# A third of block 2's first modulation on VectorE beside linear attention, and the context's second-layer path dealt in larger portions

## The chip, the cores and the metric

The kernel runs on one core of one Trainium2 chip, in one launch. The metric is the device time of the whole program in microseconds. Three runs of the kernel before took 3452.48, 3447.66 and 3446.35 us, median 3447.66 us.

## The reference, cut to what matters

Block 1 is a mixing block (differential attention and gated linear attention, called GLA below, then a router and 32 experts), whose shifts and scales come from `w_ada`. Block 2 has two layers. Each computes a modulation vector from the conditioning for the main tokens (512) and one for the context tokens (256), and both then pass through the same weights:

```python
s_c, s_ctx = silu(c), silu(c_ctx)[None]
for i in range(2):
    mod = (s_c @ w_mod[i] + b_mod[i])[:, None, :]             # 6 x 1024 columns
    sh1, sc1, gt1, sh2, sc2, gt2 = split(mod, 6)
    mod_c = (s_ctx @ w_mod[i][:, :n_mod_c] + b_mod[i][:n_mod_c])
    h  = rms_norm(x, g_norm1[i]) * (1 + sc1) + sh1
    hc = rms_norm(ctx, g_norm1[i]) * (1 + mc[1]) + mc[0]
    p, pc = h @ w_in[i], hc @ w_in[i][...]
    ...                                                       # three attention branches, merge, MLP
```

Of `mod`, the first third (shift and scale of the first norm, columns 0 to 2047, which the kernel counts as 16 columns of 128) is what a path needs to start.

## The kernel before, in words

A matrix is split into a high and a low part (tiles `wh`, `wl`, `h`), and each product is three matmuls, L195 to L197 (`mm`). The modulations are the exception: `mods_group` (L326) multiplies the raw weights. A group is a third of a modulation, 32 matmuls (8 rows of the contraction by 4 column blocks) of 128x32 by 128x512, line L339, tile `mod`; column block j writes partitions 32j to 32j+31. The tile is copied (`modr`), transposed four times (`modt`) and added to the bias. Weights `wm` come by one 256 KB DMA a matmul on SyncE's queue, into tiles of the tag `at` (9 buffers) or `t2`.

Work is written by generators that yield a cost, and `weave` advances the one that is least far in its own time (cost divided by the stream's speed). What comes out is then put in an order on each engine when the program is built, and each engine keeps to it. Stages, by the time of the profile:

- 0 to 135 us, start: first third of block 1's modulation (mod0), norms, projections. 135 to about 270: GLA (`gla`, chains over 16 chunk steps through `S`, `gqd`, `zb`), woven with projections and with groups 1 and 2 of mod0 (`mods`, tag `at`).
- to 365: attention heads 0 to 2. With head 3 (`hd == 3`, L750) the stream `ctx` begins, which runs block 2's context path of layer 0, `path(0, 256)`, beside the rest of block 1 (project, route, experts, combine). Ahead of it stands `opening()`: group 0 of block 2's modulation of layer 0 (`mods2(0, "t2", (0,))`), which the path needs; groups 1 and 2 (`later`) follow when it is done.
- 1330 to 1450: the experts end (tile `yp`) and `combine` begins; the rest of `ctx` fills there.
- 2055 to 2431: `mlp` of `path(0, 512)`. Beside it run `mods2_cols(1, ...)`, which computes layer 1's whole modulation on VectorE, column by column (48 columns; two products of 128x512 with a running sum for each row of conditioning, L1217, tile `wc`; a column of the first 16 for both rows, of the others for one), and, once 16 columns are done, `fill`: `path(1, 256)`, which gives only keys and values of the context for layer 1 (tiles `ck`, `kv`, `mkr`, `mk`). `FILL_SPEED` and `COL_COST` set in which proportion.
- from 2431: `path(1, 512)`. Its norm (`ss` sums squares, `rs` is the inverse root, `rb` spreads it, then eight pairs of `nt` and `h`) is woven with what is left of `fill`, and its first projections take `h`.

Of the kernel before, what the change touches and what calls it, by code (L numbers as in the profile page):

```python
# [14 lines left out]
P = 128  # L15
# [15 lines left out]
FIRST = 70.0  # L31
JOIN = 75.0
NP = 3
FILL_SPEED = 0.15
COL_COST = 5.5
PRO_SPEED = 0.3
ROUTE_SPEED = 0.5

# [42 lines left out]
def weave(main, back=()):  # L81


    every = list(main) + list(back)
    for s in every:
        s.t = 0.0
    while any(not s.done for s in main) or any(s.hold for s in every):
        live = [s for s in every if not s.done]
        held = [s for s in live if s.hold]
        if held:  # L90
            live = [s for s in live if s.hold or not s.weights]
        if all(s.done for s in main):
            live = held
        yield abs(min(live, key=lambda v: v.t).step())


def drain(gen):
    for _ in gen:
        pass


def chain(*gens):
    for g in gens:
        yield from g


class Gen:
# [263 lines left out]
    def run(self):  # L371
        nc, tc = self.nc, self.tc
        one, two = "1" in self.parts, "2" in self.parts
        if one:
            xs = self.load_x(self.A["xT"], 512, "xx")
            s0 = self.cond(self.A["cc"], "mod0s")
        self.ident = self.const("c_ident")
        self.ones = self.cc(P)
        nc.vector.memset(self.ones, 1.0)
        dram = self.ctx.enter_context(tc.tile_pool(name="dram", bufs=1, space=bass.MemoryType.DRAM))  # L380
        self.xs_dram = [dram.tile([KD, P, 512], F32, name=f"xres{i}") for i in range(3)]
        self.ctx_dram = [dict(kna=dram.tile([4, P, 512], F32, name=f"kna{i}"), vna=dram.tile([2, P, 512], F32, name=f"vna{i}"),
                              kml=dram.tile([8, 96, 512], F32, name=f"kml{i}"), vml=dram.tile([2, P, 512], F32, name=f"vml{i}"))
                         for i in range(2)]
        self.v_dram = [dram.tile([512, 512], F32, name=f"vloc{i}") for i in range(2)]
        self.xctx_dram = dram.tile([KD, P, 256], F32, name="xctx")
        self.Hd = [dram.tile([512, 512], F32, name=f"Hd{c}") for c in range(2)]
        self.Id = dram.tile([1024, 1], I32, name="Id")
        self.Yd = dram.tile([NE * CAP + OVF * CAP, D], F32, name="Yd")
        ctx = []  # L390
        if two:
            place = lambda n: self.place(n)
            first = Stream(self.mods2(0, "t2", (0,), place))

            def rest():
                while not first.done:
                    yield 1
                yield from self.mods2(0, "t2", (1, 2), place)

            def opening():  # L400
                while not first.done:
                    yield first.step()

            later = Stream(rest(), 1.0, False)
            ctx = [Stream(chain(opening(), self.path(0, 256, before=later))), later]
        for s in ctx:
            s.speed = 0.5
        if two and not one:
            self.second_start()
        if one:  # L410
            project = self.front(ctx, xs, s0)
        else:
            self.xs_dram[0] = self.A["t_x"]
        if one:
            for gen, speed, held in ((project, PRO_SPEED, True), (self.route(), ROUTE_SPEED, False), (None, 0, 0),
                                     (self.experts(), CTX_SPEED, None), (self.combine(), TAIL_SPEED, None)):
                if gen is None:
                    self.branch()
                    continue
                for s in ctx:  # L420
                    s.speed = speed
                drain(weave([Stream(gen, 1.0, bool(held), (lambda: tc.high_priority(PRIOR)) if held is not None else None)], ctx))
        if two:
            self.rest = ctx
            self.fill = [Stream(self.path(1, 256), FILL_SPEED)]
            drain(self.path(0, 512))
            drain(self.path(1, 512))
        else:
            xs = self.load_x(self.xs_dram[0], 512, "xo")
            for k in range(KD):  # L430
                nc.sync.dma_start(self.out[k], xs[k])


    def front(self, ctx, xs, s0):
        nc, A, tc = self.nc, self.A, self.tc
# [84 lines left out]
        w = self.load_split(W[3], 256)  # L520
# [108 lines left out]
        def dv():  # L629
            for i in range(6):  # L630
                V[i] = self.t2("dv")
            for c in range(2):
                yield from row_tiles(6 + c, V, c * 256)

        gr = [None] * 4
        def gates():
            for i in range(4):
                gr[i] = self.t2("gr")
            for c in range(2):
                w = self.load_split(W[4 + c], 256)  # L640
                for t in range(4):
                    ps = self.mm()
                    self.rows(ps[:, :256], h, t, w)
                    self.silu2(gr[t][:, c * 256:(c + 1) * 256], ps[:, :256], 256)
                    yield 2.6 if t == 3 else -2.6
# [15 lines left out]
        def qk(hd):  # L661
            w = self.load_split(W[8 + hd], 256)
            q, k = self.pairs(2, 512, "dqk")
            kc = self.pairs(1, 256, "dkc")[0]
            for m, hl in ((0, q), (1, k)):
                ps = self.mm()
                self.colsT(ps, w, m, h)
                x = self.t2("rx")
                self.copy_act(x, ps, scale=1.0 if m else 0.125)
                yield -5.1  # L670
                pr = self.mm()
                nc.tensor.matmul(pr, rot, x, start=True, stop=True)
                t1 = self.t2("ry")
                nc.vector.tensor_tensor(t1, pr, sin, op=OP.mult)
                nc.gpsimd.tensor_tensor(x, x, cos, op=OP.mult)
                nc.vector.tensor_tensor(x, x, t1, op=OP.add)
                self.split(*hl, x)
                yield -1
            ps = self.mm()
            self.colsT(ps[:, :256], w, 1, hc)  # L680
            self.split(*kc, ps[:, :256])
            QK[hd] = q, k, kc
            yield 2.6
# [57 lines left out]
            yield 0.5  # L741

        mods = Stream(chain(*[self.mods_group(mod, s0, A["w_ada"], g, "at", lambda n: self.place(n)) for g in (1, 2)]), MOD_SPEED, False)
        self.place = self.dd
        drain(weave([Stream(gla(), 1.0, False), Stream(chain(gates(), dv(), qk(0)), 1.2)], [mods]))
        drain(mods.gen)
        self.place = self.mm
        for hd in range(4):
            drain(weave([Stream(attend(hd), 1.0, False), Stream(chain(gate_norm() if hd == 0 else (), qk(hd + 1) if hd < 3 else ()), 1.2)],
# [445 lines left out]
        self.s2 = self.cond(A["cc2"], "mod2s")  # L1195
        self.mod2 = [self.mods(A["b_mod"][L], f"mod2{L}") for L in range(2)]

    def mods2_cols(self, L, cost):

        nc = self.nc  # L1200
        bt, mod = self.mod2[L]
        junk = self.t2("junk")
        rows = [[self.load(self.at("crow")[:, :512], self.A["c2_rows"][c, h]) for h in range(2)] for c in range(2)]
        for s in rows[0] + rows[1]:
            nc.scalar.activation(junk, s, AF.Tanh, scale=0.5)
            nc.vector.scalar_tensor_tensor(s, junk, 1.0, s, op0=OP.add, op1=OP.mult)
        yield 1
        for j in range(48):
            w = [self.at("wc")[:, :512] for h in range(2)]
            for h in range(2):  # L1210
                nc.gpsimd.dma_start(w[h], self.A["w_mod_t"][j, h])
            if j == 16:
                rows.pop()
            for c, row in enumerate(rows):
                to, beg = mod[:, j, c:c + 1], bt[:, j:j + 1]
                for h in range(2):
                    nc.vector.tensor_tensor_reduce(junk, w[h], row[h], 0.5, beg, OP.mult, OP.add, to)  # L1217
                    beg = to
            self.mod2_cols = j + 1
            yield cost  # L1220

    def mods2(self, L, tag, groups=range(3), place=None):
        for g in groups:
# [12 lines left out]
    def path(self, L, n, side=None, before=None):  # L1236
# [197 lines left out]
            yield from s.gen  # L1434
        back = ()
        if lat and L == 0:
            cols, fill = Stream(self.mods2_cols(1, COL_COST), 1.0, False), self.fill[0].gen
            self.mod2_cols = 0

            def later():  # L1440
                while self.mod2_cols < 16:
                    yield 1
                yield from fill

            back = self.fill = [Stream(later(), FILL_SPEED), cols]
# [376 lines left out]
def layout(inp):  # L1822
# [3 lines left out]
    f = np.float32  # L1826
# [42 lines left out]


    A["w_mod"] = modw(x["w_mod_2"][0])
    A["w_mod_t"] = ca(x["w_mod_2"][1].T.reshape(48, P, 2, 512).transpose(0, 2, 1, 3))
    A["c2_rows"] = ca(np.repeat(np.stack([x["c_2"][0], x["c_ctx_2"]]).reshape(2, 2, 1, 512), P, 2))
    A["b_mod"] = np.stack([tiles(x["b_mod_2"][i]) for i in range(2)])
    for i in range(2):
# [104 lines left out]
```

## Time and profile before

| | us |
|---|---|
| three runs | 3452.48, 3447.66, 3446.35 |
| median | 3447.66 |
| profiled execution | 3450.65 |
| its span | 3448.7 |
| TensorE busy | 3274.5 |
| VectorE busy | 1776.7 |
| ScalarE busy | 1242.7 |

The profiled execution is 2.0 us longer than its span and 3.0 us above the median. The mean granted TensorE clock is 0.972. Busy shares are averages over the stages; a stage's limit is read from that stage.

### The profile page before, as it was taken

Reading aid. Unit: us, or ns where it says so; the run is one execution under the profiler, and the core shown is the slowest. Engines: PE = TensorE matmul, PEld = TensorE weight load, DVE = VectorE, ACT = ScalarE, POOL = GpSimd, SP = SyncE. Lnnn points to the kernel's source line nnn. Section 1 sums busy time; section 2 is a strip of 40 time slices with the busy share of each in tenths; the row PEclk is TensorE's granted clock in tenths of the full one; section 3 lists DMA queues with packets and bytes.
Section 4 is the critical chain, followed back from the end, with each engine's and each line's share of the span. In section 5 each row is a group of like instructions: output and inputs, shape, how many; then the busy total and the mean of one; then the engine's idle time right before and its main releaser. Section 6 shows DMA issues by size and latency. Waiting matters only on the chain. (4 is left out here: it accounts for less than half of the span.)

```text
span 3448.7 us, 48970 instructions
## 1 busy us (share of the span) xinstructions
PE 3274.5 (95%) x19076; PEld 2501.5 (73%) x19076; DVE 1776.7 (52%) x3430; ACT 1242.7 (36%) x2206; POOL 468.0 (14%) x648
## 2 busy tenths in 40 slices
PE   7999998999999999899999999999799999999999
PEld 4987545665566667887777777788697777778887
DVE  5337635334434335645476469944445467554443
ACT  4214414333323224344454332333334354432332
POOL 1000022112222112100010112301200001010000
PEclk9999999999999999899999999999799899999999
DMA  7341576998899997433222236833333222132332
GB/s 268 92 130 50 182 263 225 339 362 337 320 385 401 389 380 276 147 108 101 78 63 63 89 106 215 265 111 126 107 100 114 75 74 63 50 104 92 98 98 80
DMA packets 198422, 597.10 MB, mean 173 GB/s; under 512 B 32955, under 2 KB 37819, under 8 KB 198188
## 3 DMA queue, kind: packets, MB, share of 16 engines
q1 hardware_dynamic: 150812, 439.24, 36.6%
q0 software_dynamic: 47376, 154.71, 12.8%
q8 instruction: 151, 2.47, 0.3%
q14 instruction: 83, 0.68, 0.1%
HBM read 564.74 MB, written 33.29 MB: 173 GB/s over the span
## 5 line engine op out<-in xcount | busy, mean ns | idle before, releaser
L171 DVE TENSOR_TENSOR wl<-wr,wh 128x1024 fp32r<-128x1024 f32 (+1 forms) x452 | 554.2, 1229 | 487.1 <-ACT wh L170 468.9
L170 ACT ACTIVATE wh<-wr 128x1024 fp32r<-128x1024 f32 (+1 forms) x452 | 473.2, 1048 | 717.1 <-PE mm L196 529.9
L195 PE MATMUL mm<-wh,h 128*128 128x256 f32 (+1 forms) x1104 | 322.6, 293 | 10.7 <-ACT h L290 8.8
L196 PE MATMUL mm<-wl,h 128*128 128x256 f32 (+1 forms) x1104 | 319.7, 290 | 8.7 <-DVE wl L171 8.7
L197 PE MATMUL mm<-wh,h 128*128 128x256 f32 (+1 forms) x1104 | 318.3, 289 | 0.0
L195 PE MATMUL mm<-f,wh 128*128 128x512 f32 (+1 forms) x768 | 275.8, 361 | 6.7 <-ACT uu L1461 3.4
L195 PE MATMUL mm<-u,wh 128*128 128x512 f32 (+1 forms) x768 | 274.0, 357 | 2.8 <-ACT u L170 2.5
L197 PE MATMUL mm<-f,wl 128*128 128x512 f32 (+1 forms) x768 | 275.0, 359 | 1.0 <-DVE wl L171 1.0
L197 PE MATMUL mm<-u,wl 128*128 128x512 f32 (+1 forms) x768 | 273.0, 356 | 2.7 <-DVE wl L171 2.7
L196 PE MATMUL mm<-f,wh 128*128 128x512 f32 (+1 forms) x768 | 275.0, 359 | 0.0
L196 PE MATMUL mm<-u,wh 128*128 128x512 f32 (+1 forms) x768 | 272.8, 355 | 0.3 <-DVE u L171 0.3
L1033 PE MATMUL gu<-we,xT 128*64 128x512 f32 x1024 | 240.7, 600 | 0.7 <-ACT xT L167 0.7
L195 PEld LDWEIGHTS mm<-wh,h 128*128 128x128 f32 x1104 | 217.3, 197 | 24.4 <-ACT h L290 10.7
L196 PEld LDWEIGHTS mm<-wl,h 128*128 128x128 f32 x1104 | 217.7, 197 | 13.5 <-DVE wl L171 8.9
L197 PEld LDWEIGHTS mm<-wh,h 128*128 128x128 f32 x1104 | 216.8, 197 | 7.3 <-issue 6.4
L195 PE MATMUL pg<-h,wh 128*128 128x512 f32 (+1 forms) x576 | 213.9, 371 | 7.4 <-ACT th L1800 2.8
L197 PE MATMUL pg<-h,wl 128*128 128x512 f32 (+1 forms) x576 | 210.0, 365 | 0.0
L196 PE MATMUL pg<-h,wh 128*128 128x512 f32 (+1 forms) x576 | 209.6, 364 | 0.0
L368 ACT ACTIVATE p<-S,mx 128x768 f32<-128x768 f32 (+2 forms) x192 | 144.5, 755 | 99.1 <-DVE mx L1506 37.2
L195 PEld LDWEIGHTS mm<-f,wh 128*128 128x128 f32 x768 | 147.2, 192 | 34.0 <-ACT uu L1461 5.0
L1033 PEld LDWEIGHTS gu<-we,xT 128*64 128x64 f32 x1024 | 72.1, 137 | 133.0 <-issue 121.6
L195 PEld LDWEIGHTS mm<-u,wh 128*128 128x128 f32 x768 | 146.2, 191 | 30.1 <-issue 5.7
(514 smaller groups left out, 6481.7 us busy)
## 6 DMA issues: line engine op xcount, KB each, us to landing
we<-in_expert_w_gate_dram SPq DMA_DIRECT2D x128, 512.0 KB, 8.1
we<-in_expert_w_up_dram SPq DMA_DIRECT2D x128, 512.0 KB, 7.8
we<-in_expert_w_down_dram SPq DMA_DIRECT2D x128, 512.0 KB, 9.2
wr<-in_ffn_w_dram SPq DMA_DIRECT2D x128, 512.0 KB, 3.7
wr<-in_w_in_dram SPq DMA_DIRECT2D x120, 512.0 KB, 3.9
wr<-in_ffn_w_dram POOLq DMA_DIRECT2D x64, 512.0 KB, 6.8
wr<-in_w_in_dram POOLq DMA_DIRECT2D x58, 512.0 KB, 5.5
wm<-in_w_mod_dram SPq DMA_DIRECT2D x96, 256.0 KB, 5.4
```

The source lines that it names most:

```text
L170: self.nc.scalar.activation(hi, src, AF.Copy)
L171: self.nc.vector.tensor_tensor(lo, src, hi.bitcast(F32), op=OP.subtract)
L195: mm(out, ah, bh, start=i == 0, stop=False)
L196: mm(out, ah, bl, start=False, stop=False)
L197: mm(out, al, bh, start=False, stop=i == n - 1)
L368: self.nc.scalar.activation(p, s, AF.Exp, bias=m, accum_out=sm)
L1033: nc.tensor.matmul(gu[64 * e:64 * e + 64, m * 512:m * 512 + 512], xT[k // 4][:, o:o + 64], w[e][kk], start=k == 0, stop=k == KD - 1)
```

## The change

Group 0 of block 2's layer 0 modulation leaves TensorE and the `ctx` stream. It is computed by `mods2_cols` with the first 16 columns of a transposed copy of the weights (`w_mod_t0`), on VectorE, as background of the GLA stage, with its DMAs on SyncE's queue. Four `crow` tiles (the conditioning rows) stay in the `at` buffers while it runs, and each column takes two more (`wc`). `path(0, 256)` starts as soon as `hd == 3`, and groups 1 and 2 with it. For layer 1, `FILL_SPEED` goes from 0.15 to 0.19 and `COL_COST` from 5.5 to 6.0, with the first 16 columns at three quarters of that.

```diff
--- before.py
+++ after.py
@@ -31,8 +31,8 @@
 FIRST = 70.0
 JOIN = 75.0
 NP = 3
-FILL_SPEED = 0.15
-COL_COST = 5.5
+FILL_SPEED = 0.19
+COL_COST = 6.0
 PRO_SPEED = 0.3
 ROUTE_SPEED = 0.5
 
@@ -389,20 +389,8 @@
         self.Yd = dram.tile([NE * CAP + OVF * CAP, D], F32, name="Yd")
         ctx = []
         if two:
-            place = lambda n: self.place(n)
-            first = Stream(self.mods2(0, "t2", (0,), place))
-
-            def rest():
-                while not first.done:
-                    yield 1
-                yield from self.mods2(0, "t2", (1, 2), place)
-
-            def opening():
-                while not first.done:
-                    yield first.step()
-
-            later = Stream(rest(), 1.0, False)
-            ctx = [Stream(chain(opening(), self.path(0, 256, before=later))), later]
+            later = Stream(self.mods2(0, "t2", (1, 2), lambda n: self.place(n)), 1.0, False)
+            ctx = [Stream(self.path(0, 256, before=later)), later]
         for s in ctx:
             s.speed = 0.5
         if two and not one:
@@ -741,9 +729,10 @@
             yield 0.5
 
         mods = Stream(chain(*[self.mods_group(mod, s0, A["w_ada"], g, "at", lambda n: self.place(n)) for g in (1, 2)]), MOD_SPEED, False)
+        cols = Stream(self.mods2_cols(0, range(16), 4.0, nc.sync) if ctx else iter(()), 1.0, False)
         self.place = self.dd
-        drain(weave([Stream(gla(), 1.0, False), Stream(chain(gates(), dv(), qk(0)), 1.2)], [mods]))
-        drain(mods.gen)
+        drain(weave([Stream(gla(), 1.0, False), Stream(chain(gates(), dv(), qk(0)), 1.2)], [mods, cols]))
+        drain(chain(mods.gen, cols.gen))
         self.place = self.mm
         for hd in range(4):
             drain(weave([Stream(attend(hd), 1.0, False), Stream(chain(gate_norm() if hd == 0 else (), qk(hd + 1) if hd < 3 else ()), 1.2)],
@@ -1195,7 +1184,8 @@
         self.s2 = self.cond(A["cc2"], "mod2s")
         self.mod2 = [self.mods(A["b_mod"][L], f"mod2{L}") for L in range(2)]
 
-    def mods2_cols(self, L, cost):
+    def mods2_cols(self, L, js, cost, queue):
+
 
         nc = self.nc
         bt, mod = self.mod2[L]
@@ -1205,10 +1195,10 @@
             nc.scalar.activation(junk, s, AF.Tanh, scale=0.5)
             nc.vector.scalar_tensor_tensor(s, junk, 1.0, s, op0=OP.add, op1=OP.mult)
         yield 1
-        for j in range(48):
+        for j in js:
             w = [self.at("wc")[:, :512] for h in range(2)]
             for h in range(2):
-                nc.gpsimd.dma_start(w[h], self.A["w_mod_t"][j, h])
+                queue.dma_start(w[h], self.A[f"w_mod_t{L}"][j, h])
             if j == 16:
                 rows.pop()
             for c, row in enumerate(rows):
@@ -1217,7 +1207,7 @@
                     nc.vector.tensor_tensor_reduce(junk, w[h], row[h], 0.5, beg, OP.mult, OP.add, to)
                     beg = to
             self.mod2_cols = j + 1
-            yield cost
+            yield cost * 0.75 if j < 16 else cost
 
     def mods2(self, L, tag, groups=range(3), place=None):
         for g in groups:
@@ -1434,7 +1424,7 @@
             yield from s.gen
         back = ()
         if lat and L == 0:
-            cols, fill = Stream(self.mods2_cols(1, COL_COST), 1.0, False), self.fill[0].gen
+            cols, fill = Stream(self.mods2_cols(1, range(48), COL_COST, nc.gpsimd), 1.0, False), self.fill[0].gen
             self.mod2_cols = 0
 
             def later():
@@ -1869,7 +1859,8 @@
 
 
     A["w_mod"] = modw(x["w_mod_2"][0])
-    A["w_mod_t"] = ca(x["w_mod_2"][1].T.reshape(48, P, 2, 512).transpose(0, 2, 1, 3))
+    for i in range(2):
+        A[f"w_mod_t{i}"] = ca(x["w_mod_2"][i].T.reshape(48, P, 2, 512).transpose(0, 2, 1, 3)[:(16, 48)[i]])
     A["c2_rows"] = ca(np.repeat(np.stack([x["c_2"][0], x["c_ctx_2"]]).reshape(2, 2, 1, 512), P, 2))
     A["b_mod"] = np.stack([tiles(x["b_mod_2"][i]) for i in range(2)])
     for i in range(2):
```

In GLA, TensorE's order holds the matmuls of mod0's groups 1 and 2 (`mod` from `wm` and `mod0ss`) between projections (`mm`). Before:

```order
L196 MATMUL mm_1632<-wl_1629,h_14_264 128x256
L197 MATMUL mm_1632<-wh_1628,h_14_264 128x256
L339 MATMUL mod_1189<-wm_1660,mod0ss 32x512
L339 MATMUL mod_1189<-wm_1663,mod0ss 32x512
L339 MATMUL mod_1189<-wm_1666,mod0ss 32x512
L339 MATMUL mod_1189<-wm_1669,mod0ss 32x512
L339 MATMUL mod_1189<-wm_1672,mod0ss 32x512
L339 MATMUL mod_1189<-wm_1675,mod0ss 32x512
L339 MATMUL mod_1189<-wm_1678,mod0ss 32x512
L339 MATMUL mod_1189<-wm_1681,mod0ss 32x512
L195 MATMUL mm_1684<-wh_1622,h_0_257 128x256
L196 MATMUL mm_1684<-wl_1623,h_0_257 128x256
```

and now, at a like place:

```order
L196 MATMUL mm_1757<-wl_1694,h_8_261 128x256
L339 MATMUL mod_1189<-wm_1740,mod0ss 32x512
L197 MATMUL mm_1757<-wh_1693,h_8_261 128x256
L195 MATMUL mm_1757<-wh_1693,h_10_262 128x256
L196 MATMUL mm_1757<-wl_1694,h_10_262 128x256
L197 MATMUL mm_1757<-wh_1693,h_10_262 128x256
L195 MATMUL mm_1757<-wh_1693,h_12_263 128x256
L196 MATMUL mm_1757<-wl_1694,h_12_263 128x256
L197 MATMUL mm_1757<-wh_1693,h_12_263 128x256
L339 MATMUL mod_1189<-wm_1743,mod0ss 32x512
L195 MATMUL mm_1757<-wh_1693,h_14_264 128x256
```

The eight matmuls of a run stand apart now, with other matmuls between them. Over the program, mod0's last 64 matmuls stand in 11 runs before and in 41 now; the 64 of block 2's groups 1 and 2 in 44 before and in 50 now.

VectorE in GLA's output part (`gqd` is the decayed query and key of a chunk, L596 and L597, now L584 and L585). Before:

```order
L596 TENSOR_TENSOR gqd_1717<-gqd_1717,gq_1020 128x128
L596 TENSOR_TENSOR gqd_1717<-gqd_1717,gq_1021 128x128
L597 TENSOR_TENSOR gqd_1717<-gqd_1717,gkT_1022 128x128
L597 TENSOR_TENSOR gqd_1717<-gqd_1717,gkT_1023 128x128
L596 TENSOR_TENSOR gqd_1727<-gqd_1727,gq_1020 128x128
L597 TENSOR_TENSOR gqd_1727<-gqd_1727,gkT_1022 128x128
L596 TENSOR_TENSOR gqd_1727<-gqd_1727,gq_1021 128x128
L597 TENSOR_TENSOR gqd_1727<-gqd_1727,gkT_1023 128x128
```

and now:

```order
L584 TENSOR_TENSOR gqd_1790<-gqd_1790,gq_1020 128x128
L584 TENSOR_TENSOR gqd_1790<-gqd_1790,gq_1021 128x128
L1207 ISA junk_1214,cc_1003<-wc_1749,crow_1215,cc_1003 128x512
L1207 ISA cc_1003 128x1
L585 TENSOR_TENSOR gqd_1790<-gqd_1790,gkT_1022 128x128
L1207 ISA junk_1214,cc_1003<-wc_1750,crow_1217,cc_1003 128x512
L1207 ISA cc_1003 128x1
L585 TENSOR_TENSOR gqd_1790<-gqd_1790,gkT_1023 128x128
L1207 ISA junk_1214,cc_1003<-wc_1749,crow_1219,cc_1003 128x512
L1207 ISA cc_1003 128x1
L584 TENSOR_TENSOR gqd_1800<-gqd_1800,gq_1020 128x128
L1207 ISA junk_1214,cc_1003<-wc_1750,crow_1221,cc_1003 128x512
```

The 64 products of the columns, each with its `ISA cc` that reads the sum, stand between the steps of the chain, all ahead of attention head 0.

TensorE at the end of `mlp(0, 512)`, where `path(1, 512)` begins. Before, from the last `ss` on:

```order
L262 MATMUL ss_21895<-cc_91,sq_21563 128x1
L262 MATMUL ss_21895<-cc_91,sq_21881 128x1
L217 MATMUL ckt_21946<-cc_91,ckn_21947 128x128
L217 MATMUL rb_21978<-cc_91,rs_21905 128x128
L217 MATMUL ckt_21946<-cc_91,ckn_21950 128x128
L217 MATMUL rb_21978<-cc_91,rs_21905 128x128 x3
L195 MATMUL kv_21967<-wh_21960,ck_0_21945 128x512
L196 MATMUL kv_21967<-wl_21961,ck_0_21945 128x512
L195 MATMUL kv_22057<-wh_22050,ck_0_21945 128x512
L197 MATMUL kv_21967<-wh_21960,ck_0_21945 128x512
L196 MATMUL kv_22057<-wl_22051,ck_0_21945 128x512
L197 MATMUL kv_22057<-wh_22050,ck_0_21945 128x512
```

and now, from the last products of the MLP (`u`) on:

```order
L196 MATMUL mm_22062<-u_15_21257,wh_22028 128x512
L197 MATMUL mm_22062<-u_14_21256,wl_22029 128x512
L217 MATMUL mkt_22094<-cc_91,mkr_21907 96x128
L217 MATMUL mkt_22094<-cc_91,mkr_21908 96x128
...
L217 MATMUL mkt_22118<-cc_91,mkr_21908 96x128
L262 MATMUL ss_22136<-cc_91,sq_21736 128x1
L262 MATMUL ss_22136<-cc_91,sq_22089 128x1
...
L217 MATMUL rb_22160<-cc_91,rs_22146 128x128 x4
L195 MATMUL mm_22213<-wh_22203,h_0_22128 128x256
L196 MATMUL mm_22213<-wl_22204,h_0_22128 128x256
L195 MATMUL mm_22239<-wh_22203,h_0_22128 128x256
```

Both `ckt`, the 12 `kv` matmuls and 8 of the 16 `mkt` have moved ahead of the MLP's end. The other 8 `mkt` stand ahead of `ss`, and after `rb` the projections of `h` follow with nothing between.

## Rows read from the trace of the kernel before

**Rows 1.** The page: span, and busy time of TensorE (us, share, instructions).

```profile
span 3448.7 us, 48970 instructions
...
PE 3274.5 (95%) x19076; PEld 2501.5 (73%) x19076; DVE 1776.7 (52%) x3430; ACT 1242.7 (36%) x2206; POOL 468.0 (14%) x648
```

**Rows 2.** By stage: stretch, each engine's us (instructions), granted clock, DMA share.

```profile
135.00:262.00 127.00, 126.03 (x940) 104.37 (x941) 44.70 (x127) 24.46 (x55) 1.30 (x3) 0.97 0.37 118
262.00:365.00 103.00, 100.30 (x593) 78.31 (x592) 72.08 (x125) 46.63 (x92) 10.57 (x8) 1.00 0.16 49
365.00:424.00 59.00, 53.92 (x265) 28.02 (x264) 38.95 (x96) 21.88 (x46) 2.59 (x3) 0.97 0.71 250
```

**Rows 3.** The modulation tiles alone, by stage, same columns, two records a matmul.

```profile
0.00:50.00 50.00, 14.52 (x64) 2.55 (x64) 0.69 (x1) 0.97 0.89 312
50.00:365.00 315.00, 18.60 (x128) 3.65 (x128) 1.36 (x2) 0.99 0.33 101
365.00:424.00 59.00, 21.82 (x64) 3.04 (x64) 0.69 (x1) 0.97 0.71 250
424.00:560.00 136.00, 47.36 (x128) 6.54 (x128) 1.36 (x2) 0.98 0.70 245
```

**Rows 4.** TensorE in order of time: start, us, line, out<-in, records; two pieces.

```profile
145.38 1.06 PE L339 MATMUL mod<-wm,mod0ss 128*32 128x512 f32 x8
...
369.50 1.90 PE L339 MATMUL mod<-wm,mod2ss 128*32 128x512 f32 x10
...
391.65 1.04 PE L339 MATMUL mod<-wm,mod2ss 128*32 128x512 f32 x2
```

**Rows 5.** VectorE groups in 2062 to 2237: shape, count | busy, mean ns | idle before.

```profile
L1217 DVE CUSTOM_DVE_ANT_0 junk<-wc,crow,cc 128x512 f32<-128x512 f32 x127 | 95.9, 755 | 7.5 <-DMA wc<-in_w_mod_t_dram 5.5
L171 DVE TENSOR_TENSOR wl<-wr,wh 128x1024 fp32r<-128x1024 f32 x32 | 39.0, 1220 | 0.0
L1217 DVE DVE_READ_ACCUMULATOR2_ANT cc<- 128x1 f32 x127 | 10.4, 82 | 0.0
```

**Rows 6.** DMA issues in 130 to 290: count, KB each, median us to landing.

```profile
wm<-in_w_ada_dram SPq DMA_DIRECT2D x38, 256.0 KB, 4.2
```

**Rows 7.** TensorE in order of time at the start of the block's end (combine).

```profile
1417.83 0.88 PE L195 MATMUL mm<-wh,h 128*128 128x256 f32 x2
1427.36 0.58 PE L196 MATMUL mm<-wl,h 128*128 128x256 f32 x1 [8.65 <-DVE wl L171]
```

**Rows 8.** Two parts of block 2's first MLP, columns as in Rows 2.

```profile
2062.00:2237.00 175.00, 169.21 (x766) 139.06 (x765) 166.82 (x369) 54.09 (x73) 56.30 (x99) 1.00 0.73 235
2237.00:2420.00 183.00, 183.00 (x901) 155.25 (x900) 87.47 (x115) 63.68 (x81) 23.54 (x31) 1.00 0.38 123
```

**Rows 9.** TensorE in order of time from the MLP's end.

```profile
2430.93 0.39 PE L197 MATMUL mm<-u,wl 128*128 128x512 f32 x1
...
2447.33 0.58 PE L195 MATMUL mm<-wh,h 128*128 128x256 f32 x1 [4.23 <-ACT h L290]
...
2452.34 0.66 PE L217 MATMUL mkt<-cc,mkr 128*96 128x128 f32 x2 [1.08 <-DVE mk L176]
...
2480.15 0.28 PE L196 MATMUL mm<-wl,h 128*128 128x256 f32 x1
2480.27 0.28 PE L197 MATMUL mm<-wh,h 128*128 128x256 f32 x1
...
2481.39 0.39 PE L195 MATMUL mm<-wh,h 128*128 128x256 f32 x1 [0.36 <-ACT kraw L167]
```

**Rows 10.** VectorE in order of time, same stretch.

```profile
2466.06 0.17 DVE L229 SCALAR_TENSOR_TENSOR rs<-rs,rs 128x8 f32<-128x8 f32 x1
...
2476.21 0.74 DVE L291 SCALAR_TENSOR_TENSOR h<-nt,cc,h 128x512 fp32r<-128x512 f32 x1
2476.87 0.74 DVE L283 SCALAR_TENSOR_TENSOR nt<-xr,cc,rb 128x512 f32<-128x512 f32 x1
```

**Rows 11.** Busy time in 20 us of the same stretch, columns as in Rows 2.

```profile
2460.00:2480.00 20.00, 11.65 (x43) 8.94 (x44) 15.06 (x37) 7.77 (x15) 6.84 (x13) 0.50 0.34 106
```

## The prediction

> **What bounds the kernel now.** I read the page's busy times first: TensorE works 3274.5 of 3448.7 us, 95% [rows 1]. So nearly every microsecond of matmul added or removed is a microsecond of time, unless it falls into one of the few places where TensorE stands still. Then the busy time by stage: in GLA (135 to 262 us) TensorE works 126.03 of 127 us while VectorE works 44.70; from 262 to 365 it works 100.30 of 103 although VectorE works 72.08; from 365 to 424, attention head 3, it works 53.92 of 59 [rows 2]. The reader is to see that VectorE has room in GLA, and that TensorE has none. Last I read the time order at the end of block 2's first MLP, where TensorE has gaps: between its last product at 2430.93 us and the third tile of the next projections at 2481.39 us it is mostly waiting [rows 9], and in 2460 to 2480 it works 11.65 of 20 us at a granted clock of 0.50, which is the lower of its two levels, 1.2 GHz [rows 11].
>
> **What a modulation matmul costs.** A lone one (two records) takes 1.04 us; four in a row, on four different column blocks, take 1.06 us together; five take 1.90 [rows 4]. So the price goes by rounds: each begun four of a run cost one round. The sums by stage bear this out. The 64 matmuls from 50 to 365 us stand in 18 rounds and take 18.60 us, 1.03 a round; group 0 of block 2 (365 to 424 us) has 32 matmuls in 21 rounds and takes 21.82 us, 1.04; groups 1 and 2 have 45 rounds and take 47.36 us, 1.05 [rows 3]. This is the number on which the forecast turns, since the order shown above pulls the runs of mod0 apart.
>
> **The change part by part.**
>
> 1. *Group 0 of block 2's modulation leaves TensorE.* −21.8 us [rows 3], and four transposes at some 0.12 us: −22.3 us.
>
> 2. *Groups 1 and 2 of block 2* now stand in 50 rounds where they stood in 45: 5 x 1.05 = +5.2 us.
>
> 3. *mod0's groups 1 and 2 in GLA.* The `at` tag has 9 buffers; the four `crow` tiles and the columns' `wc` leave at most five for `wm`, less where columns are in flight. So the loads come singly, and the matmuls were placed singly: 64 matmuls in 45 rounds instead of 18. 27 x 1.03 = +27.9 us. TensorE has 1 us of idle time in this stage [rows 2], so nothing hides it.
>
> 4. *The columns on VectorE.* 64 products at 0.755 and 64 reads at 0.082 us [rows 5] are 53.6 us, beside GLA. VectorE comes to 44.7 + 53.6 = 98 us in about 127 + 28 = 155 us, 63%. The trace has no product between the chain's steps. Below, the cost is nothing, since TensorE has other matmuls queued; above, every product delays a chain step for which TensorE waits, 53.6 us. The nearest row is 262 to 365 us, where VectorE is 70% busy and TensorE idle for 2.7 of 103 us, 2.6% [rows 2]: 2.6% of 155 is 4 us, 1 of which is there now. I take +3 us.
>
> 5. *Loads.* The 32 `wc` loads of 256 KB enter SyncE's queue, and so does each wait for a free `at` tile; the projections' `wr` loads stand behind them. A `wm` load takes 4.2 us to land [rows 6]. Below nothing; above, each of the 41 runs waits for a load of its own, up to 4.2 us each. Tile time: 32 `wc` tiles held for some 4.2 us of landing and 4 x 0.84 us of products, 64 `wm` tiles for 4.2 and a round of 1.0, together 242 + 333 = 575 us over five tiles, 115 of 155 us. It fits, without much room. I take +1 us. The Trainium skill's page "DMA: Bandwidth & Descriptors" (section "Anatomy of one DMA — SWDGE (gpsimd) path") puts a transfer at 2.0 us and its bytes over 436 GB/s, so an estimate of 2.6 us for 256 KB; by that the tiles would be busy for some 85 us and the second rival below would be unlikely. The trace's 4.2 us, on SyncE's queue, is longer, and I go by it.
>
> 6. *Head 3, projection, route.* In head 3 TensorE idles 5.1 of 59 us although modulation matmuls fill there [rows 2]. Now the context path's own work fills in. At best the 5.1 us go, −5; at worst they double, +5. In the new order fewer matmuls stand in the route's norm, so I take +2 us.
>
> 7. *The block's end.* Counted in the two orders, 48 of the context path's 128x256 matmuls move ahead of the last expert's output. At 0.12 us each (2480.15 to 2480.27) [rows 9] that is +5.8 us ahead of the chain that ends block 1. Behind it, TensorE waits 8.65 us for VectorE's weight split `wl` [rows 7], so fewer fillers cost nothing there, and two splits at 1.22 us [rows 5] fewer stand ahead in VectorE's queue, −2.4. Sum +3.4 us; the ends are −2.4 and +5.8.
>
> 8. *Layer 1's context keys and values move into the MLP.* Before, 12 `kv`, 2 `ckt` and 16 `mkt` stood behind the MLP, each pair of `mkt` at 1.08 us of wait and 0.66 of work, 1.74 us [rows 9], and between them the norm's steps, so that the third projection tile came 50.5 us after the MLP's last product. Now four pairs remain: 4 x 1.74 = 7.0; `ss`, `rb` and the hand-overs between engines, an estimate of 3; 12 steps of `rs` at 0.20 us, 2.4; 16 steps `nt` and `h` at 0.70, 11.2 [rows 10]. The third tile then starts after 23.6 us, call it 24: −26.5 us. What moved into the MLP costs TensorE there 12 x 0.24 (twice the 0.12) and 10 x 0.12 us, +4.1; it is fully busy in the MLP's second part, 183.00 of 183 [rows 8], so this counts. The clock was back at its upper level when the third tile started at 2481.39; after a gap that stays, the first few us of dense work will run at the lower one, +2 us (the ends are 0 and the 6 us that four such us and a slow norm would cost). Sum −20.4 us. The columns' order hardly changes at the MLP's start, where VectorE works 166.82 of 175 us [rows 8]; I cost that edit at 0, −3 to +3.
>
> Sum: −22.3 + 5.2 + 27.9 + 3 + 1 + 2 + 3.4 − 20.4 = −0.2 us. Against the profiled execution, 3450.65, this is 3450.4; against the median, which is 3.0 lower, 3447.4 us. I forecast 3447 us: two gains of about 20 us, one of them eaten by the runs that come apart.
>
> **Rivals.**
>
> *A. The waits I added do not come (faster).* The sum without terms 4 to 7 and the 2 us of clock is −0.2 − 3 − 1 − 2 − 3.4 − 2 = −11.6: 3436 us. For it: TensorE was idle for 1 us only in GLA, and its order now has matmuls between any two dependent steps; each of its rounds is longer in fact than a short matmul, so VectorE gets more time. Against: VectorE goes from a third busy to two thirds, and one in-order queue serves both. If also the MLP's first part loses its 5.8 us of idle time (175 less 169.21, [rows 8]), it is 3430 us.
>
> *B. Loads for `at` tiles hold TensorE in GLA (slower).* One mechanism: a modulation matmul stands in TensorE's order at the place where the builder thought its tile would have landed; if the tile came free late, because VectorE had not yet finished the column in it, TensorE stops, and the projections behind it with it. With 0.5 us for each of the 41 runs it is +20: 3467 us. It decides from 0.25 us a run (10 us). For it: 115 of 155 us of tile time, a queue in which a waiting load holds the next. Against: no wait of TensorE for a load in this stage now, and the DMA engines are 37% busy [rows 2].
>
> *C. The change does not do what it says at the MLP's end:* the moved keys and values wait for one another inside the MLP as they did behind it. Then 8 `mkt` and the `kv` would give back some 4 x 1.08 + 2 x 1.1, 6.5 us: 3454 us, inside my range.
>
> **How the numbers follow.** My forecast, with C, has a chance of 0.41, A 0.34, B 0.25. The likeliest one's own range is 3439 to 3456 us. What a measurement of this kernel can tell from no change is about 0.2%, 6.9 us, so the bounds are 3440.8 and 3454.6. Faster: A and a tail of the forecast, 0.34 + 0.03 = 0.37; slower: B and a tail, 0.25 + 0.03 = 0.28; within: 0.35. The range for the time goes from beyond A, 3427, to B, 3468.
>
> **What would show it.** Modulation tiles alone from 50 to about 395 us: 46 us of TensorE where there were 18.60, and none of block 2's group 0 behind it; were it 20 to 30, runs would overlap with their neighbours, and the time would be 20 us lower. Waits of TensorE for `wm` or for GLA's tiles in that stretch: a few us by the forecast, over 10 in B. At the MLP's end, the third projection tile some 24 us after the last product; if over 35, term 8 is wrong. I am wrong altogether if block 1 ends earlier than before by 10 us or more, or if VectorE's products delay GLA by more than the rounds do.

## The result, and the profile after

The changed kernel takes 3492.49 us, the median of four runs (3490.51 to 3492.86); the kernel before took 3449.97 in four (3446.35 to 3452.48). The ratio is 1.012, with a 95% interval of 1.0107 to 1.0133. The change made it slower by 42.5 us, where 3447 was forecast and 3468 was the range's upper end.

The page of the changed kernel, to be laid beside [rows 1]:

```profile
span 3488.7 us, 48984 instructions
...
PE 3305.0 (95%) x19008; PEld 2515.9 (72%) x19008; DVE 1825.5 (52%) x3560; ACT 1244.5 (36%) x2210; POOL 463.9 (13%) x648
```

TensorE has 68 records fewer (two to an fp32 modulation matmul) and works 30.5 us longer: fewer matmuls, and more time. To see where, the program is cut at instructions that both kernels have, and each is given its start in the two traces (`go` is GLA's output, `gu` the first product of an expert, `f` and `u` feed the MLP's two products; the stage's forecast is the sum of the prediction's terms there):

| TensorE comes to | before, us | after, us | later by | forecast of the stage | what the stage did |
|---|---|---|---|---|---|
| last `go` (end of GLA) | 250.0 | 281.6 | 31.6 | +31.9 | +31.6 |
| head 3 | 361.2 | 396.6 | 35.4 | 0 | +3.8 |
| first `gu` (first expert) | 599.5 | 653.4 | 53.9 | -15.1 | +18.5 |
| first `f` of block 2's first MLP | 2040.3 | 2095.6 | 55.3 | +3.4 | +1.4 |
| last `u` of that MLP | 2430.9 | 2501.0 | 70.1 | +4.1 | +14.8 |
| third projection tile | 2481.4 | 2525.2 | 43.8 | -24.5 | -26.3 |
| last `u` of the program | 3439.8 | 3479.7 | 40.0 | 0 | -3.8 |

One stage stands out. From head 3 to the first expert 15 us were to be won, and 18.5 were lost. Busy time by stage in the kernel before, cut at the same places (columns as in [rows 2]):

```profile
361.00:412.30 51.30, 46.22 (x250) 26.42 (x246) 35.10 (x83) 20.65 (x43) 3.16 (x3) 0.97 0.66 223
412.30:599.50 187.20, 175.31 (x843) 103.55 (x842) 92.44 (x260) 55.39 (x90) 40.43 (x60) 0.97 0.69 242
2050.00:2431.30 381.30, 375.29 (x1769) 313.08 (x1767) 266.02 (x498) 127.83 (x171) 81.69 (x132) 1.00 0.54 174
```

and in the changed one, GLA and heads 0 to 2 first, then head 3, then projection and route, the MLP, and last two short stretches:

```profile
135.00:282.00 147.00, 143.97 (x894) 100.62 (x895) 83.25 (x244) 23.64 (x56) 1.05 (x2) 0.97 0.51 158
282.00:396.60 114.60, 111.27 (x631) 83.09 (x630) 76.42 (x137) 46.98 (x91) 10.69 (x9) 1.00 0.17 54
396.60:463.20 66.60, 59.36 (x254) 33.38 (x252) 42.16 (x105) 23.03 (x50) 8.15 (x9) 0.82 0.55 176
463.20:653.40 190.20, 169.43 (x818) 107.72 (x818) 85.82 (x235) 56.45 (x89) 37.16 (x58) 0.93 0.59 206
2105.50:2501.30 395.80, 384.95 (x1789) 319.70 (x1788) 282.09 (x557) 137.00 (x198) 85.12 (x144) 0.98 0.54 173
...
420.00:450.00 30.00, 29.46 (x100) 13.96 (x100) 15.58 (x44) 6.61 (x14) 3.28 (x4) 0.73 0.46 143
560.00:600.00 40.00, 27.53 (x130) 19.79 (x129) 20.30 (x52) 11.04 (x16) 9.09 (x16) 0.79 0.55 203
```

Head 3 with projection and route takes 256.8 us where it took 238.5. TensorE idles 28.0 us there (7.2 + 20.8) where it idled 17.0, and it is busy 7.3 us longer although 22.3 us of group 0 are gone. Part of that is the granted clock, at which the same matmuls last longer: 0.82 in head 3 where it was 0.97, and 0.93 behind it where it was 0.97. In 420 to 450 us TensorE is busy nearly throughout and gets 0.73 of its clock.

The modulation tiles alone, by stage, to be laid beside [rows 3]:

```profile
0.00:50.00 50.00, 14.45 (x64) 2.71 (x64) 0.69 (x1) 0.93 0.87 304
50.00:396.00 346.00, 48.01 (x128) 6.82 (x128) 1.37 (x2) 0.99 0.37 115
396.00:424.00 28.00, 0.00 (x0) 0.00 (x0) 0.00 (x0) 0.79 0.55 177
424.00:580.00 156.00, 55.62 (x128) 7.22 (x128) 1.37 (x2) 0.95 0.59 205
```

In GLA they take 48.01 us (46 forecast, 18.60 before). The third line is the one not foreseen: from the start of head 3 to 424 us there is no modulation matmul at all, and the granted clock is 0.79. In the kernel before the first one of block 2 stood at 369.50, inside the head [rows 4]. TensorE of the changed kernel there, in order of time (start, us, and in brackets the idle time before and who ended it):

```profile
407.14 0.96 PE L203 MATMUL S<-dqk,dqk 64*128 64x512 f32 x3 [2.13 <-ACT p L368]
410.44 1.54 PE L217 MATMUL tp<-cc,p 128*128 128x128 f32 x6 [0.84 <-DVE p L695]
420.54 1.51 PE L217 MATMUL tp<-cc,p 128*128 128x128 f32 x6 [2.68 <-DVE p L695]
426.36 1.92 PE L339 MATMUL mod<-wm,mod2ss 128*32 128x512 f32 x4
...
442.65 1.05 PE L339 MATMUL mod<-wm,mod2ss 128*32 128x512 f32 x4
```

The head's softmax chain is now waited for, and a run of two modulation matmuls (x4: two records each) lasts 1.92 us at the lower of the two levels (1.2 GHz) and 1.05 sixteen us later at the upper (2.4 GHz). Why the matmuls come so late is in SyncE's queue (start of an issue group, us from its first to its last, line, count). The changed kernel:

```profile
373.06 32.43 SPq L185 DMA_DIRECT2D wr<-in_w_out_dram  x3
405.59 6.03 SPq L154 DMA_DIRECT2D x<-in_ctx2T_dram  x8
411.66 18.35 SPq L154 DMA_DIRECT2D wm<-in_w_mod_dram  x16
```

and the kernel before:

```profile
336.52 1.41 SPq L185 DMA_DIRECT2D wr<-in_w_out_dram  x2
337.99 26.13 SPq L154 DMA_DIRECT2D wm<-in_w_mod_dram  x8
```

Before, eight `wm` loads were issued ahead of the next `wr` (a projection's weights): the first four by 339.8 us, the last at 363.8, so six during head 2 and two as head 3 began. Now the first `wm` stands behind three `wr`, of which the second and third are issued at 404.08 and 405.17, when VectorE has freed their tiles, and behind the path's `x`, the context's input. The Trainium skill's page "DMA: Bandwidth & Descriptors" (section "Issuing engines are not separate DMA queues") says that issuing from several engines saves only the sequencer's issue time, usually small beside the transfer. No run here moves loads to another engine. What the rows show is another cost of one queue: behind a `wr` that waited 31 us for its tile, the loads that followed it on SyncE's queue were issued only after it.

In the route the cover (matmuls that fill TensorE's waits) is gone as well. The modulation is done at 569.85 us (`modt`), and the context path's keys (`tq`) and then the route's own norm (`ss`, `rb`, and the router's product `lgT` behind it) follow bare:

```profile
569.85 0.60 PE L217 MATMUL modt<-cc,modr 128*128 128x128 f32 x4
...
577.17 1.29 PE L217 MATMUL tq<-cc,kraw 128*128 128x128 f32 x4 [3.87 <-DVE kraw L1284]
579.33 1.12 PE L217 MATMUL tq<-cc,kraw 128*128 128x128 f32 x4 [0.87 <-DVE nk L176]
581.25 3.55 PE L262 MATMUL ss<-cc,sq 128*128 128x1 f32 x16 [0.80 <-DVE nk L176]
587.32 1.09 PE L217 MATMUL rb<-cc,rs 128*128 128x128 f32 x4 [2.52 <-DVE rs L230]
590.06 2.78 PE L812 MATMUL lgT<-h,router 128*36 128x512 f32 x3 [1.66 <-ACT h L285]
```

In the kernel before, the same norm stood among modulation matmuls and the path's projections (`mm`), without a wait of TensorE from `ss` to `rb`, and the modulation ended behind it:

```profile
508.09 1.72 PE L262 MATMUL ss<-cc,sq 128*128 128x1 f32 x14
...
510.44 1.04 PE L339 MATMUL mod<-wm,mod2ss 128*32 128x512 f32 x2
...
515.81 0.27 PE L217 MATMUL rb<-cc,rs 128*128 128x128 f32 x1
515.83 0.36 PE L197 MATMUL mm<-wh,h 128*128 128x256 f32 x1
...
548.09 0.60 PE L217 MATMUL modt<-cc,modr 128*128 128x128 f32 x4
```

At the other end of the program, the MLP and the next projections (to be laid beside [rows 9]):

```profile
2332.43 0.28 PE L197 MATMUL mm<-wh,h 128*128 128x256 f32 x1
2337.74 1.20 PE L217 MATMUL tq<-cc,kraw 128*128 128x128 f32 x4 [5.03 <-DVE kraw L1284]
...
2501.03 0.39 PE L197 MATMUL mm<-u,wl 128*128 128x512 f32 x1
...
2506.05 3.54 PE L262 MATMUL ss<-cc,sq 128*128 128x1 f32 x16 [1.14 <-DVE mk L176]
2512.12 1.09 PE L217 MATMUL rb<-cc,rs 128*128 128x128 f32 x4 [2.52 <-DVE rs L230]
...
2525.16 0.39 PE L195 MATMUL mm<-wh,h 128*128 128x256 f32 x1 [0.36 <-ACT kraw L167]
```

The third tile comes 24.1 us after the last product (24 forecast, 50.5 before). The new wait for `kraw` at 2337.74, 5.03 us inside the MLP, was not foreseen.

### The profile page after: what moved, and what is told of

Its sections match the earlier page's. It is cut to its first block, busy times and chain, and to the rows that moved or that the text cites. A ratio compares the mean times of both kernels' runs of the same rounds, so it can differ in the third digit from the quotient of the medians.

```text
span 3488.7 us, 48984 instructions
## 1 busy us (share of the span) xinstructions
PE 3305.0 (95%) x19008; PEld 2515.9 (72%) x19008; DVE 1825.5 (52%) x3560; ACT 1244.5 (36%) x2210; POOL 463.9 (13%) x648
## 3 DMA queue, kind: packets, MB, share of 16 engines
q1 hardware_dynamic: 151388, 440.28, 36.5%
```

## The experiments

Each kernel was timed against the kernel before on the same chip; the chips differ between some runs, so the ratio compares them best. The expectations call runs 1 to 10 e1_fill, e2_cols, e3_t2, e6_nogroup0, e9_group1, e10_filler, e11_head2, e12_order, e13_after_group1 and e14_slow. "Portions" are `FILL_SPEED`, `COL_COST` and the three quarters of the last part of the change. The stretch "head 3 to expert" runs from the start of head 3 to the first `gu`: 238.5 us before, 256.8 after.

**1. The portions alone, in the kernel before.**

```diff
-FILL_SPEED = 0.15
-COL_COST = 5.5
+FILL_SPEED = 0.19
+COL_COST = 6.0
-            yield cost
+            yield cost * 0.75 if j < 16 else cost
```

> The kernel before, with the two portion numbers of the change alone (FILL_SPEED 0.19, COL_COST 6.0, the first 16 columns at three quarters). By the trace of after, the MLP takes 14.5 us longer with the keys and values in it and the stretch behind it 26.4 us less: 12 to 14 us faster than before, 3436 us. By the prediction's term 8 (-20.4): 3430 us. If these gains hang on the other half of the change: no difference from before.

3437.82 us against 3452.31, ratio 0.9955 (0.9938 to 0.9972): 14 us faster. The MLP ends 20.4 us later (2451.33 for 2430.93), the third tile starts 5.9 us earlier (2475.46). Of the 20.4 us, 5.4 were there when the MLP began (2045.69 for 2040.34): the MLP took 15.0 us longer and the stretch behind it 26.3 less. The profiled execution was the longest of the four, 3445.63 us. So the portions are a gain by themselves, smaller than term 8, and the loss lies in the rest.

**2. The change without the portions.**

```diff
-FILL_SPEED = 0.19
-COL_COST = 6.0
+FILL_SPEED = 0.15
+COL_COST = 5.5
-            yield cost * 0.75 if j < 16 else cost
+            yield cost * 0.75 if j < 16 and L == 0 else cost
```

> The kernel after, with the portions of before (0.15, 5.5): the move of the modulation alone. By the trace of after, which is 54 us late at the first expert: 54 to 56 us slower than before, 3505 us. By the prediction's terms 1 to 7 (+20.2): 3470 us.

3505.63 us, 1.0149 (1.0131 to 1.0167): 53 us slower. First expert at 655.9 us, 56.4 later than before.

**3. As 2, with the columns' tiles in `t2`,** so that the loads of mod0 keep the `at` buffers and its matmuls stay in runs.

```diff
-self.load(self.at("crow")[:, :512], ...)
+self.load((self.at if L else self.t2)("crow")[:, :512], ...)
-            w = [self.at("wc")[:, :512] for h in range(2)]
+            w = [(self.at if L else self.t2)("wc")[:, :512] for h in range(2)]
```

> As e2_cols, but the columns' tiles (crow, wc) come from the t2 buffers, so the nine at buffers stay with mod0: 28 rounds stand in the order where e2_cols has 53. Theory 'runs': 25 rounds at 1.03 us, 26 us less than e2_cols, and GLA ends within 5 us of before. Rival 'VectorE': the 64 products and the load queue delay GLA, so e3_t2 stays within 8 us of e2_cols and GLA still ends some 25 us late.

3483.28 us, 1.0084 (1.0066 to 1.0102), 22 us under run 2, where the theory gave 26. The modulation tiles in GLA take 20.71 us instead of run 2's 48.90, and GLA ends at 262.3, 12 us later than before, where the theory allowed 5; two waits for VectorE's gate step (`gr`) make 6.0 us of that and are put down to the columns, which share its queue (this wasn't tested by itself). 31 us of the loss remain: the stretch from head 3 to the expert takes 258.5 us.

**4. As 2, without the columns:** group 0 is left out of the program, and its shift and scale are set to zero.

```diff
-cols = Stream(self.mods2_cols(0, range(16), 4.0, nc.sync) if ctx else iter(()), 1.0, False)
+cols = Stream(self.mods2_cols(0, range(16), 4.0, nc.sync) if False else iter(()), 1.0, False)
...
+        self.nc.gpsimd.memset(self.mod2[0][1][:, 0:16, :], 0.0)
```

> As e2_cols without any columns: group 0 of block 2's layer 0 modulation is left out (its shift and scale are zero), nothing is added to GLA. Theory 'cover': the 32 matmuls stood where TensorE otherwise waits and its clock falls, so from head 3 to the first expert it takes up to 18 us longer than before, as in after; total 3455 to 3470 us. Rival, the prediction's term 1: 21 rounds at 1.04 less, 17 us faster than before, 3433 us.

3471.31 us, 1.0057 (1.0038 to 1.0076). This is the run that breaks the prediction. GLA is as before (last `go` at 249.9), 32 matmuls are gone and nothing stands in their place, and the kernel is 19 us slower. Busy time from head 3 to the first `mt` (the transposes that begin the projection), and on to the first expert:

```profile
361.00:428.90 67.90, 60.36 (x255) 34.37 (x253) 42.21 (x105) 23.03 (x50) 8.14 (x9) 0.80 0.56 173
428.90:619.00 190.10, 169.56 (x816) 107.75 (x816) 85.86 (x235) 56.35 (x89) 36.23 (x57) 0.93 0.59 206
```

They are the changed kernel's two lines over again, 258.0 us with the clock at 0.80 and 0.93. Neither GLA nor the columns are needed for this loss.

**5. Group 1 takes group 0's place.** As 3 with the new portions, and `opening()` of the kernel before put back, with group 1 in it and group 2 in `later`.

```diff
-            later = Stream(self.mods2(0, "t2", (1, 2), lambda n: self.place(n)), 1.0, False)
-            ctx = [Stream(self.path(0, 256, before=later)), later]
+            place = lambda n: self.place(n)
+            first = Stream(self.mods2(0, "t2", (1,), place))
+            def rest():
+                ...
+                yield from self.mods2(0, "t2", (2,), place)
+            ...
+            ctx = [Stream(chain(opening(), self.path(0, 256, before=later))), later]
```

> As e3_t2 with the portions of the change (worth 14 us), and group 1 of block 2's modulation ahead of the context path, as group 0 stood there before: head 3 has 32 modulation matmuls beside it again, route has 32 fewer than before. Theory 'cover': head 3 takes the 51 us of before again, not 68, the stretch from head 3 to the first expert falls from 258 to about 235 us; 3469 - 23 = 3446 us. Rival 'early path' (what costs is that 48 matmuls of the path come ahead of the experts): only the 6 us of these come back, 3463 us.

3427.53 us against 3452.82, 0.9925 (0.9908 to 0.9941): faster than both kernels, by 25 and by some 65 us. Again 32 matmuls fewer on TensorE, but now they are worth their time:

```profile
371.80:423.10 51.30, 46.12 (x247) 26.32 (x245) 35.26 (x83) 20.63 (x43) 3.15 (x3) 0.97 0.67 226
423.10:591.10 168.00, 154.68 (x773) 100.16 (x772) 90.48 (x253) 55.01 (x90) 39.36 (x60) 0.97 0.62 218
```

Head 3 takes the 51.3 us of the kernel before at its clock of 0.97, and 19.2 us are saved behind it. The stretch is 219.3 us, 39 less than run 3's 258.5, where the theory gave 23: it had counted head 3 and the 48 matmuls of the path, not what the route would win. The path also starts later here, so the run by itself doesn't part the filler from the later start.

**6. As 4, with the 32 matmuls put back behind the path's start,** at the head of `later`; their result isn't used.

```diff
-later = Stream(self.mods2(0, "t2", (1, 2), lambda n: self.place(n)), 1.0, False)
+later = Stream(self.mods2(0, "t2", (0, 1, 2), lambda n: self.place(n)), 1.0, False)
```

> As e6_nogroup0 (path starts at once, its shift and scale are zero), but the 32 matmuls of group 0 run on TensorE with groups 1 and 2, their result unused. Theory 'cover': they fall where TensorE waits now, in route, and cost little: within 8 us of e6_nogroup0's 3471 us, although they are 22 rounds of 1.04 us. Rival, every round costs its time: 3471 + 23 = 3494 us.

3485.92 us, 1.0094 (1.0077 to 1.0111), 15 us over run 4 and between the two expectations. The matmuls alone, late, do not mend head 3:

```profile
363.40:431.50 68.10, 61.17 (x254) 35.00 (x252) 42.18 (x105) 23.05 (x50) 8.15 (x9) 0.77 0.56 173
431.50:636.20 204.70, 193.40 (x886) 111.33 (x886) 87.51 (x240) 56.57 (x89) 36.81 (x57) 0.95 0.65 232
```

There they cost 15 of the 22 us that their rounds take, so they cover little. What counts is where filler stands.

**7. As 5, without the opening, the stream started one head earlier.**

```diff
-                        ctx if hd == 3 else ()))
+                        ctx if hd >= 2 else ()))
```

> As e3_t2 with the portions of the change, and the context stream starts beside head 2, not head 3, which only a path that need not wait for group 0 can do. Theory 'cover': the path's norm is then done earlier, so matmuls stand beside head 3 and 144 of the path's are ahead of the experts; from head 2 on 10 to 20 us less than e3_t2 less 14 (3469 us): 3449 to 3459 us. Rival: the path and the modulation cost VectorE and ScalarE in heads 2 and 3, where the softmax sets the pace: 3469 us or more.

3441.93 us, 0.996 (0.9942 to 0.9978): some 27 us better than with the start at head 3 (3469, which is run 3 less run 1's gain), more than either theory gave. Head 3 takes 90.7 us, as the context's work runs in it, and what follows 164.7. The run doesn't separate the theories; its surplus wasn't traced further.

**8. As 7 with the start at head 3 again, and `later` ahead of the path in the list,** so that its loads are issued first.

```diff
-            ctx = [Stream(self.path(0, 256, before=later)), later]
+            ctx = [later, Stream(self.path(0, 256, before=later))]
```

> As e3_t2 with the portions of the change (3469 us by the runs so far), but the stream of groups 1 and 2 stands ahead of the path's in the list, so that their first eight loads are issued on SyncE's queue before the path's loads and before the two projection loads that wait for a buffer, as in before. The path still starts at once. Theory 'queue': head 3 lacks matmuls because those loads stand behind waiting ones; it takes 51 to 54 us instead of 68, total 3453 us or less. Rival 'share': the path takes turns from the modulation and from VectorE in head 3, which stays at 65 us or more, total 3465 us or more.

3461.72 us, ten runs, 1.0025 (1.0015 to 1.0034).

```profile
373.00:431.00 58.00, 49.61 (x258) 29.01 (x256) 41.85 (x106) 23.25 (x50) 8.17 (x9) 0.91 0.62 193
431.00:620.10 189.10, 167.48 (x814) 107.94 (x812) 85.69 (x233) 56.19 (x89) 37.74 (x58) 0.93 0.58 202
```

With the first `wm` loads issued early again, at 349.83 us, head 3 falls from 68.4 us (run 3) to 58.0 and its clock rises from 0.78 to 0.91. The part behind it stays at 189 us. So 10.4 of the 17.1 us that head 3 had lost in run 3 come back, between what the two theories gave, and the route's loss is a second thing. The edit also changes the order in which the streams take turns, so the queue isn't shown apart from that; the 6.7 us that head 3 still lacks were not traced.

**9. The changed kernel with group 1 ahead of the path,** the edit of run 5 alone.

> The kernel after (columns in the at buffers, new portions) with one edit: group 1 ahead of the context path. If the parts add up: after's 3492 less the 39 us that e9_group1 saved between head 3 and the first expert, 3453 us, and GLA still 30 us late. If the cover that e9_group1 regained was due to its earlier end of GLA: 3470 us or more.

3453.19 us against 3452.70, ten runs, 1.0002 (0.9992 to 1.0011): no change, 39 us under the changed kernel.

```profile
397.50:448.30 50.80, 46.02 (x247) 26.41 (x245) 35.04 (x83) 20.63 (x43) 3.15 (x3) 0.97 0.68 227
448.30:614.30 166.00, 152.68 (x773) 98.56 (x772) 90.51 (x253) 55.02 (x90) 39.34 (x60) 0.98 0.63 221
```

Its stretch is 216.8 us, 21.7 under the kernel before, and GLA still ends at 282.3. The total is the prediction's own sum, -0.2 us, in a kernel that keeps the cover, but by luck in part: by this trace GLA and heads 0 to 2 give +36.5 us (31.9 forecast), the stretch -21.7 (-15.1), the MLP and what stands behind it -11.3 (-20.4), the rest -4.4 (3.4).

**10. As 8, with the context streams slower during the projection,** so that the modulation lasts into the route.

```diff
-PRO_SPEED = 0.3
+PRO_SPEED = 0.17
```

> As e12_order (path at once, groups 1 and 2 first in the list), with PRO_SPEED 0.17 for 0.3: during project the path and the modulation are dealt in smaller portions, so that 48 of the path's matmuls fall behind the first expert again and the last modulation matmuls stand around the router's norm (rb, lgT), where e12_order has none. Theory 'cover in route': the stretch from the first mt to the first expert falls from e12_order's 189 us to about 172, total 3445 us. Rival 'early start': what costs there is that the path begins beside head 3 (VectorE, ScalarE and queues), so the stretch stays at 183 us or more and the total at 3455 us or more.

3446.35 us against 3450.57, ten runs, 0.998 (0.9969 to 0.999), 15 us under run 8.

```profile
373.00:436.00 63.00, 54.11 (x265) 32.48 (x261) 41.76 (x106) 23.25 (x50) 8.75 (x10) 0.84 0.56 177
436.00:608.70 172.70, 154.53 (x764) 98.18 (x762) 82.98 (x229) 52.71 (x83) 33.69 (x52) 0.95 0.62 215
```

One number of the planner takes 16.4 us out of projection and route (189.1 to 172.7), 5 of which head 3 gives back. Some 6 of the 16.4 are the 48 matmuls of the path that move behind the first expert again (48 at 0.12 us); 3.4 are idle time (21.6 to 18.2); the rest, 7.2, is busy time, at a clock of 0.95 for 0.93. The route's loss was thus in good part cover spent too early; the same number also slows the path, and the two aren't parted.

## Why the prediction was wrong

The step that failed is term 6, with the part of term 1 that hangs on it. Term 1 counted group 0 as 22.3 us of TensorE that go. But these matmuls also did a service: their loads were issued ahead of the stop in SyncE's queue, so they stood ready in head 3 while TensorE would have waited for the softmax, and they pushed groups 1 and 2 and the path so far back that these covered the route's norm. Term 6 looked at that place, saw 5.1 us of idle time "although modulation matmuls fill there", and set +2 us, at most +5, for losing them; it had no term for the clock there.

The stage was forecast at -15.1 us and measured at +18.3 by the windows (+18.5 in the table), a miss of 33.4. From the rows it comes to:

- 9.0 us of idle time: 11.0 more, where 2 were allowed for.
- 5.8 us for 48 matmuls of the path which now stand ahead of the first expert. The prediction had these, but in term 7, for a later stage.
- 18.6 us of busy time, a remainder (7.3 - (-22.3 + 5.2) - 5.8). A granted clock of 0.82 and 0.93 means that some 51 us of this stage are at the lower level (0.36 of 66.6 and 0.14 of 190.2); 0.97 meant some 14 before. In the parts of the stage whose granted clock is 0.50, TensorE works 41.7 us now and 11.5 before. If all of that takes twice as long there, the clock cost 15.1 us more: an estimate, and an upper one. What the other 3.5 us are stays open.

Run 4 shows the whole loss without the rest of the change, and runs 5 and 9 undo it with filler ahead of the path. Runs 8 and 10 part head 3 from the route: with loads issued early, 10.4 of head 3's 17.1 us come back; with modulation and path dealt out later, 16.4 us of the route's.

The prediction also says under term 6 that "the context path's own work fills in". It doesn't in head 3: its loads of `x` were issued at 405.59 us, 9 us after the head began, and its first steps are a norm, itself a chain between engines.

Point by point:

- Term 3, the runs of mod0 that come apart: right. GLA ended 31.6 us later where terms 3 to 5 gave 31.9, and in run 3, with the runs whole again, GLA ended 20.6 us earlier than in run 2. TensorE idles 3.0 us in GLA, 2.9 of it for `wm`; rival B, which needed 10 us and more there, is not what happened.
- Term 4, the columns: 6.0 us of waits in run 3, where 3 were taken. In the changed kernel no wait of TensorE for VectorE shows in GLA.
- Term 2 is within the stage that failed, and isn't seen apart. Term 7: +1.4 us for 3.4, but not as it was added up: its 5.8 us fell in the stage before, so -2.4 was left of it, and +1.4 came; what made the difference wasn't traced.
- Term 8 behind the MLP: right, 24.1 us for 24, -26.3 in all. Inside the MLP it was mis-sized: 4.1 us forecast, 14.8 measured, 14.5 of it in the two windows above. There the moved matmuls account for 5.9 (`kv` 3.9, `mkt` 1.4, `ckt` 0.6), idle time for 4.8 (the two waits ahead of `tq` are 5.9, others 1.1 less), and the remaining 3.8 are put down to matmuls that last longer: in 2330 to 2350 us the clock is 0.83. Rival C named this place; the wait, though, is of the path's keys, not of `mkt`. Run 1 shows the same sizes without the move of group 0 (+15.0 and -26.3), and -14 us in all where term 8 gave -20.4.
- Heads 0 to 2 took 3.8 us more, and what follows the third tile 3.8 less; no term foresaw these and no run explains them.

The sign was open in the prediction and the range's upper end rested on rival B alone. No rival let the cover go: the mechanism was seen as a 5 us matter and not made a case of its own. That "slower" had a chance at all was for rival B's reason, which did not come.

## What to carry to other kernels

Work that fills an engine's waits may not be worth its own duration when it is removed. Before taking it off the busiest engine, list the waits that it covers, and put other independent work in the very same place, in the order of the engine and of the queue that loads it; run 9 did only that, and the loss of 42 us was gone, with GLA still some 32 us late. And price a run of packed matmuls by how it will stand in the new order, which came to 48 us here where 46 were forecast.

## What was not expected of the hardware

- A stage lost about as much to the granted clock as to the waits themselves, perhaps more (up to 15.1 us by the estimate above, beside 11.0): 28.0 us of idle time in 256.8 went with a clock of 0.82 and 0.93, 17.0 in 238.5 with 0.97. The Trainium skill's page "TensorE: Matmul & The Clock Gate" (section "What's actually happening") says that the throttled level is the default and that activity releases it; the rows agree: 0.79 from 396 to 424 us, where head 3's waits of 0.8 to 2.7 us stand, and the upper level at 442.65, after TensorE had worked without a wait since 420.54.
- A run of two modulation matmuls takes 1.92 us at the lower level (426.36) and 1.05 at the upper (442.65), so what a round costs depends on the level that the matmuls before it left.
